# Copies of k on a second queue, logs summed earlier, half of the squares on another engine: a four-part edit of an attention and convolution trunk

## The chip, the cores and the metric

The kernel runs on one core of a Trainium2 chip. A core has TensorE (PE: matmuls, with results in eight PSUM banks of 128 x 512 float32), VectorE (DVE), ScalarE (ACT), GpSimd (POOL) and SyncE (SP), which here only issues DMAs; each engine works through its own instructions in order and waits on semaphores. Sixteen DMA engines move the data. The metric is the device time of one execution in microseconds (us), the median of several runs.

## The reference

Two layers over a sequence of 512 tokens with 1024 channels, all float32. Layer 0 mixes by attention with a forget gate, layer 1 by a short convolution; each layer then has a squared-ReLU MLP (4096 wide) and a gated embedding. Cut to what the change touches:

```
def rmsnorm(x, g):
    return x * rsqrt(mean(x * x) + 1e-6) * g

def fox_attention(h, w_in, b_f, w_out):          # h = rmsnorm(x, g[0])
    q, k, v, f_logit = split(h @ w_in)           # 16 heads of 64, and 16 gates
    c = cumsum(log_sigmoid(f_logit + b_f))       # over the 512 tokens
    s = (q / 8) @ k.T + c[query] - c[key]        # causal: -1e30 above the diagonal
    return (softmax(s) @ v) @ w_out
```

## The kernel before

All matmuls are made from a split of each float32 operand into a high and a low part: ScalarE writes the high part (`wh`, `xh`, `kh`, `hTh`) and VectorE the difference (`wl`, `xl`, `kl`, `hTl`); `mm3` then does three matmuls, high by high, high by low, low by high. Weights come by SyncE's queue into 14 buffers `raw` in a fixed order (`fetch`); a load waits until the splits of the weight 14 places before it have read its buffer.

The start of layer 0 goes like this. TensorE first makes v and the gates' logits from the raw x (chunk 0: 256 columns of v and the 16 gates; chunk 1: 512 columns; `values`: the last 256), with the norm applied afterwards: `inverse` takes the squares of token-major x (`xc`), gives `rs[t] = (mean + eps) ** -0.5` of each block t of 128 tokens, and `r_d`, its diagonal, from which `rows` makes the norm of every column. `logits` adds the gates' bias `b_f`, `logs` makes log sigmoids, and `sums_of_logs` their running sums by matmuls into `ps_c`. VectorE copies them out (`c_T`), makes `neg_c`, and SyncE writes that to memory. `normed_x` scales the two halves of x and splits them into `hTh` and `hTl`.

From these `project(i)` makes k and then q of a pair of heads. The scores of a head need k stacked twice, as high and low parts on 64 partitions each: a DMA copies `kh` and `kl` to the other half of the partitions (line 546), four copies for a pair. `bias(h)` loads `neg_c` of head h, one row for all partitions, in four DMAs (`prr`, `pr`, `prr`, `prl`, for the four blocks of queries, of 128 to 512 columns), which the scores are added to. After `project(0)` and most of the first half of `project(1)` the loop over heads begins: `scores` (lines 574 and 575), exponentials on ScalarE, transposes (`turn`), values (`mix`), with the projections of later pairs between them.

Up to the end of chunk 1 and `normed_x` the order of all engines is written out by hand; from `values` on a scheduler that works with estimated times sets it. DMAs tell of their landing on eight semaphores, `DMAHW0` to `DMAHW7`, which the scheduler gives out in turn, whichever queue issues the DMA; one that gets a semaphore waits until the DMA before it on that semaphore has landed.

Of the kernel before, what the change touches and what calls it, by code (L numbers as in the profile page):

```python
# [8 lines left out]
F32 = mybir.dt.float32  # L9
# [59 lines left out]
def trunk(ctx: ExitStack, tc, x, xT, pT, g, gT, wv, wqk, bf, wo, wci, wcq, cw, wco, wup, wdn, wpp, wpg, out):  # L69
# [16 lines left out]
    def stat(name, n=1, dtype=F32):  # L86
        return small.tile([P, n], dtype, tag=f"st{n}", name=name, bufs=32 if n == 1 else 8)
# [64 lines left out]
    def fetch(upto):  # L152
        while len(fetched) < min(upto, len(loads)):
            n = len(fetched)
            raw = raws.tile([P, S], F32, tag="raw", name=f"raw{n}")
            fetched.append(raw)
            src = loads[n]
            nc.sync.dma_start(raw[:, : src.shape[-1]], src)
# [164 lines left out]
    def stats(t, xs, name):  # L323
        return rstd([squares(xs[n][:, :S], f"{name}_q{n}_{t}") for n in range(2)], f"{name}_r{t}")
# [53 lines left out]
    def load_x(name, t):  # L378
        xs = [page(f"{name}{t}_{n}") for n in range(2)]
        for n in range(2):  # L380
            nc.sync.dma_start(xs[n][:, :S], x[t * P : (t + 1) * P, n * S : (n + 1) * S])
        return xs
# [29 lines left out]
    def attention(hT, raw_x, b_f, warm, work, by_hand):  # L412
# [31 lines left out]
        def sums_of_logs(tri):  # L444
            ps_c = bank("ps_c")
            for b in range(NB):
                for half in (lf.hi, lf.lo):
                    nc.tensor.matmul(
                        ps_c[:H, b * P :], half[:, b * H : (b + 1) * H], tri[:, : S - b * P],
                        start=b == 0 and half is lf.hi, stop=b == NB - 1 and half is lf.lo,  # L450
                    )
            c_T = page("c_T")
            nc.vector.tensor_copy(c_T[:H, :S], ps_c[:H, :])
            for b in range(NB):
                n = (b + 1) * P
                t = page(f"neg_c{b}")
                nc.vector.tensor_scalar(
                    out=t[:H, :n], in0=c_T[:H, :n], scalar1=c_T[:H, b * P : b * P + 1],
                    scalar2=-1.0, op0=ALU.subtract, op1=ALU.mult,
                )  # L460
                nc.sync.dma_start(neg_c[b, :, :n], t[:H, :n])
# [36 lines left out]
        def keep_values(c, t, ps):  # L498

            c0, width = V_CHUNKS[c]  # L500
            splits = []
            for c1 in range(0, min(width, D - c0), 256):
                i = (c0 + c1) // 256
                vs[t][i] = page(f"v{t}_{i}", F32R)
                src = ps[:, c1 : c1 + 256].rearrange("p (i e d) -> p i e d", e=2, d=HD)
                block = vs[t][i].rearrange("p (i r) -> p i r", i=2)
                for e in range(2):
                    hi = block[:, :, 192 * e : 192 * e + HD]
                    lo = block[:, :, 64 + 64 * e : 128 + 64 * e]
                    splits.append((hi, lo, src[:, :, e, :]))  # L510
            for hi, _, src in splits:
                nc.scalar.mul(hi, src, rs[t])
            for hi, lo, src in splits:
                nc.vector.scalar_tensor_tensor(
                    out=lo, in0=src, scalar=rs[t], in1=hi.bitcast(F32),
                    op0=ALU.mult, op1=ALU.subtract,
                )
# [3 lines left out]
        def project(i):  # L521

            heads = [[page(f"{n}{i}_{e}", F32R) for n in ("qs", "kh", "kl")] for e in range(2)]
            stacked[i] = heads
            for s in (1, 0):
                ps = bank(f"qk{i}_{s}")
                for k in range(KT):
                    mm3(
                        ps, narrow("qk", i, k=k, c=s * P),
                        hT.at(lambda h: h[:, k, :]), k == 0, k == KT - 1,  # L530
                    )
                    if k < KT - 1:
                        yield
                for e in range(2):
                    a, b = slice(64 * e, 64 * e + 64), slice(64 - 64 * e, 128 - 64 * e)
                    q, kh, kl = heads[e]
                    if s == 0:
                        nc.scalar.mul(q[a, :S], ps[a, :], HD**-0.5)
                        nc.vector.scalar_tensor_tensor(
                            out=q[b, :S], in0=ps[a, :], scalar=HD**-0.5,  # L540
                            in1=q[a, :S].bitcast(F32), op0=ALU.mult, op1=ALU.subtract,
                        )
                    else:
                        split(kh[a, :S], kl[a, :S], ps[a, :])
                        for h in (kh, kl):
                            nc.sync.dma_start(h[b, :S].bitcast(F32), h[a, :S].bitcast(F32))
                yield

        def bias(h):
# [144 lines left out]
        r_d = page("r_d")  # L694

        def inverse(t):
            rs[t] = stats(t, first_x[t], name)
            nc.gpsimd.tensor_scalar(
                out=r_d[:, t * P : (t + 1) * P], in0=ident, scalar1=rs[t], scalar2=None,
                op0=ALU.mult,  # L700
            )
# [10 lines left out]
        def normed_x(n, r_rows):  # L712

            halves = [raw_x[t][n][:, :S].rearrange("p (j c) -> p j c", j=4) for t in range(NB)]

            def low(t):
                to = lambda u: u[:, 4 * n : 4 * n + 4, t * P : (t + 1) * P]
                split(to(hT.hi), to(hT.lo), halves[t])

            for t, h in enumerate(halves):  # L720
                r = r_rows[:, t * P : (t + 1) * P].unsqueeze(1).to_broadcast([P, 4, P])
                nc.vector.tensor_tensor(out=h, in0=h, in1=r, op=ALU.mult)
                if t:
                    low(t - 1)
            low(NB - 1)

        with tc.manual_schedule(engines={E.PE, E.DVE, E.Activation, E.Pool, E.SP}):
            work(9)
            banks_v = {(0, t): bank(f"v0_{t}") for t in range(NB)}

            def halves(c, *at):
                for t, n in at:
                    if (c, t) not in banks_v:
                        banks_v[c, t] = bank(f"v{c}_{t}")
                    part(c, banks_v[c, t], t, n)

            split_x(0, 0)
            prepare(4)
            halves(0, (0, 0))
            split_x(0, 1)  # L740
            split_x(1, 0)
            halves(0, (1, 0))
            prepare(KT)
            fetch(2 * KT)
            first_x = [load_x("xc", t) for t in range(NB)]
            nc.sync.dma_start(b_f, bf[0:1, :].partition_broadcast(P))
            fetch(2 * KT + 4)
            halves(0, (0, 1))
            split_x(1, 1)
            halves(0, (1, 1))  # L750
            for t in (2, 3):
                for n in range(2):
                    split_x(t, n)
                    halves(0, (t, n))
            tri, ones = page("tri", F32R), page("ones")
            nc.gpsimd.memset(ones[:, :S], 1.0)
            nc.gpsimd.affine_select(
                out=ones[:, :S], in_=ones[:, :S], compare_op=ALU.is_ge, fill=0.0, base=0,
                pattern=[[1, S]], channel_multiplier=-1,
            )  # L760
            nc.vector.tensor_copy(tri[:, :S], ones[:, :S])
            prepare(KT + 4)
            halves(1, (0, 0), (1, 0))
            prepare(2 * KT)
            halves(1, (0, 1), (1, 1))
            for t in range(NB):
                inverse(t)
            halves(1, (2, 0))
            r_rows = rows()
            halves(1, (2, 1), (3, 0), (3, 1))  # L770
            for two in ((0, 1), (2, 3)):
                for t in two:
                    logits(t, banks_v[0, t])
                for t in two:
                    keep_values(0, t, banks_v[0, t])
                prepare(2 * KT + 4)
            steps = logs()
            next(steps)
            keep_values(1, 0, banks_v[1, 0])
            next(steps)  # L780
            keep_values(1, 1, banks_v[1, 1])
            next(steps)
            normed_x(0, r_rows)
            keep_values(1, 2, banks_v[1, 2])
            normed_x(1, r_rows)
            keep_values(1, 3, banks_v[1, 3])
        for t in range(NB):
            values(t)
            if t == 1:
                sums_of_logs(tri)  # L790
                bias(0)
                bias(1)
        for _ in project(0):
# [517 lines left out]
```

## Time and profile before

| | us |
|---|---|
| median of 3 runs (lowest, highest) | 1232.28 (1232.04, 1233.59) |
| the profiled execution | 1232.33 |
| its span, first to last instruction | 1230.4 |
| TensorE busy | 1209.3 (98%) |
| VectorE busy | 928.4 (75%) |
| ScalarE busy | 694.1 (56%) |
| GpSimd busy | 657.7 (53%) |

Times in the views count from the start of the span. A row of the timeline has the start, the time taken, engine, line, operation, output and inputs, and in brackets the idle time before it with what ended it; `SPq` is SyncE's queue, where the time is that of the issue and not of the transfer. A row of waits has the engine that waited, what it waited for, the total, how often, and the longest.

### The profile page before, as it was taken

How to read it: one execution, taken by the hardware profiler on the slowest of the kernel's cores; microseconds unless marked ns; L12 is line 12 of the kernel's file. 1: busy time of each engine (PE TensorE's matmuls, PEld its weight loads, DVE VectorE, ACT ScalarE, POOL GpSimd, SP SyncE). 2: the span in 40 equal slices, each digit the busy share in tenths (PEclk: the TensorE clock that was granted, in tenths of full speed). 3: DMA queues.
4: the chain of work that ended last, by engine and by line, in shares of the span. 5: the costliest groups of instructions: out<-in, count | busy, mean ns of one | idle time of the engine just before them, and what ended most of it. 6: DMA issues, size and time to landing. Idle time of an engine off the chain costs nothing.

```text
span 1230.4 us, 18747 instructions
## 1 busy us (share of the span) xinstructions
PE 1209.3 (98%) x6175; PEld 1030.8 (84%) x6175; DVE 928.4 (75%) x1462; ACT 694.1 (56%) x1473; POOL 657.7 (53%) x620
## 2 busy tenths in 40 slices
PE   9969999999999999999999999999999999999997
PEld 8858888798888888888889999989888888888886
DVE  5848888666787768869777798766776887669873
ACT  7747778647644644465567444445756345635551
POOL 2016566235877787866213255315677777778310
PEclk9979999999999999999999999999999999999999
DMA  9455554442443234328232132542422443245401
GB/s 317 138 149 165 154 168 132 143 167 66 124 138 94 83 97 137 120 62 287 80 104 86 52 100 98 155 154 96 129 73 73 138 137 94 61 121 169 174 8 61
DMA packets 87313, 150.83 MB, mean 123 GB/s; under 512 B 10352, under 2 KB 18080, under 8 KB 87216
## 3 DMA queue, kind: packets, MB, share of 16 engines
q1 hardware_dynamic: 86640, 149.11, 39.1%
q8 instruction: 49, 0.80, 0.3%
q10 hardware_dynamic: 576, 0.53, 0.1%
q14 instruction: 48, 0.39, 0.1%
HBM read 139.03 MB, written 6.37 MB: 118 GB/s over the span
## 4 chain that ended last, share of the span: by engine, by line
PE 88%; DVE 3%; issue 3%; ACT 2%; POOL 2%; DMA 1%; SPq 0%; POOLq 0%; ACTq 0%; DVEq 0%
PE up L270 9%; PE up L268 9%; PE up L269 9%; PE dn L268 8%; PE dn L270 8%; PE dn L269 8%; PE v L476 2%; PE qk L269 2%; PE qk L270 2%; PE qk L268 2%; PE pg L269 2%; PE pg L268 2%; PE pg L270 2%; PE pT L590 1%; PE co L270 1%
## 5 line engine op out<-in xcount | busy, mean ns | idle before, releaser
L277 DVE TENSOR_TENSOR wl<-raw,wh 128x512 fp32r<-128x512 f32 x346 | 345.2, 1043 | 14.6 <-ACT wh L276 13.9
L269 PE MATMUL up<-hTh,wl 128*128 128x512 f32 (+1 forms) x576 | 210.2, 365 | 0.0
L270 PE MATMUL up<-hTl,wh 128*128 128x512 f32 (+1 forms) x576 | 209.6, 365 | 0.0
L268 PE MATMUL up<-hTh,wh 128*128 128x512 f32 (+1 forms) x576 | 208.7, 366 | 0.0
L276 ACT CAST wh<-raw 128x512 fp32r<-128x512 f32 x346 | 189.4, 625 | 4.5 <-DVE xd L373 4.4
L966 ACT ACTIVATE r<-up 128x512 f32<-128x512 f32 (+1 forms) x72 | 39.4, 548 | 202.8 <-PE up L270 190.0
L277 POOL TENSOR_TENSOR wl<-dn_T,wh 128x512 fp32r<-128x512 f32 x96 | 132.7, 1416 | 30.0 <-ACT wh L276 30.0
L168 POOL TENSOR_TENSOR dn_T<-raw,raw 128x512 f32<-128x512 f32 x56 | 87.9, 1581 | 68.4 <-DMA raw<-in_wdn 49.5
L269 PEld LDWEIGHTS up<-hTh,wl 128*128 128x128 f32 x576 | 108.6, 189 | 17.6
L268 PEld LDWEIGHTS up<-hTh,wh 128*128 128x128 f32 x576 | 108.6, 188 | 17.5
L270 PEld LDWEIGHTS up<-hTl,wh 128*128 128x128 f32 x576 | 108.2, 188 | 17.4
L1012 DVE TENSOR_TENSOR acc<-dn,acc 128x512 f32<-128x512 f32 x168 | 107.5, 680 | 14.4 <-PE dn L270 14.2
L168 POOL TENSOR_TENSOR dn_T<-raw,dn_T 128x512 f32<-128x512 f32 x56 | 92.5, 1652 | 2.2
L276 ACT CAST wh<-dn_T 128x512 fp32r<-128x512 f32 x112 | 61.4, 616 | 10.9 <-POOL dn_T L168 10.9
L277 DVE TENSOR_TENSOR A12l<-q,A12h 128x512 fp32r<-128x512 f32 x28 | 22.8, 814 | 53.7 <-ACT A12h L276 53.7
L1026 POOL TENSOR_TENSOR acc<-acc,acc 128x512 f32<-128x512 f32 x28 | 46.9, 1708 | 9.9 <-DVE acc L1012 9.9
L269 PE MATMUL qk<-hTh,wl 128*128 128x512 f32 x128 | 51.2, 401 | 0.0
L270 PE MATMUL qk<-hTl,wh 128*128 128x512 f32 x128 | 51.2, 401 | 0.0
L268 PE MATMUL qk<-hTh,wh 128*128 128x512 f32 x128 | 50.9, 399 | 0.0
L277 DVE TENSOR_TENSOR A11l<-q,A11h 128x256 fp32r<-128x256 f32 x28 | 23.2, 827 | 36.5 <-ACT A11h L276 36.5
L269 PE MATMUL pg<-wh,hTl 128*128 128x512 f32 x128 | 50.5, 394 | 0.0
L268 PE MATMUL pg<-wh,hTh 128*128 128x512 f32 x128 | 50.4, 394 | 0.0
(400 smaller groups left out, 3311.3 us busy)
## 6 DMA issues: line engine op xcount, KB each, us to landing
raw<-in_wup SPq DMA_DIRECT2D x128, 256.0 KB, 3.0
raw<-in_wdn SPq DMA_DIRECT2D x128, 256.0 KB, 2.9
raw<-in_wcq SPq DMA_DIRECT2D x36, 256.0 KB, 2.8
raw<-in_wqk SPq DMA_DIRECT2D x32, 256.0 KB, 4.9
raw<-in_wpg SPq DMA_DIRECT2D x32, 256.0 KB, 4.5
g<-in_g SPq DMA_DIRECT2D x22, 256.0 KB, 5.3
prl<-neg_c SPq DMA_DIRECT2D x16, 256.0 KB, 6.5
raw<-in_wo SPq DMA_DIRECT2D x16, 256.0 KB, 4.5
```

The costliest lines, as they stand in the source:

```text
L168: ins = nc.gpsimd.tensor_tensor(out=B[name], in0=B[a], in1=B[b], op=op)
L268: nc.tensor.matmul(ps, a.hi, b.hi, start=start, stop=False)
L269: nc.tensor.matmul(ps, a.lo, b.hi, start=False, stop=False)
L270: nc.tensor.matmul(ps, a.hi, b.lo, start=False, stop=stop)
L276: nc.scalar.copy(hi, src)
L277: return eng.tensor_tensor(out=lo, in0=src, in1=hi.bitcast(F32), op=ALU.subtract)
L476: nc.tensor.matmul(ps[:, : V_CHUNKS[c][1]], getattr(of_x(k, t), p), getattr(ready["v", c, k], of), start=k == 0 and p == of, stop=k == KT ...
L590: nc.tensor.transpose(ps[:, b * P : (b + 1) * P], probs[h][b][:, j * P : (j + 1) * P], ident)
L966: nc.scalar.activation(r[:, :n], ps[:, :n], AF.Relu)
L1012: ins = nc.vector.tensor_tensor(out=a, in0=banks[s], in1=a, op=ALU.add)
L1026: nc.gpsimd.tensor_tensor(out=a, in0=a, in1=acc[i, s][:, :S], op=ALU.add)
```

## The change

It has four parts.

- The four copies of k of the first pair of heads (`i == 0`) are issued by ScalarE and no longer by SyncE.
- `sums_of_logs`, which stood behind `values(1)`, stands ahead of the second half of `normed_x`, in the stretch that is ordered by hand.
- The load of `b_f` stands ahead of the eight loads of token-major x.
- Of the two squares of each block, one stays on ScalarE (`squares`) and one goes to VectorE (`products`, with eps inside); VectorE adds the two, and GpSimd makes the power as before.

```diff
@@ project(i), s == 1
                         for h in (kh, kl):
-                            nc.sync.dma_start(h[b, :S].bitcast(F32), h[a, :S].bitcast(F32))
+                            eng = nc.sync if i else nc.scalar
+                            eng.dma_start(h[b, :S].bitcast(F32), h[a, :S].bitcast(F32))
@@
         def inverse(t):
-            rs[t] = stats(t, first_x[t], name)
+            half = lambda n: first_x[t][n][:, :S]
+            v = stat(f"{name}_v{t}")
+            q = squares(half(0), f"{name}_q0_{t}"), products(half(1), f"{name}_q1_{t}")
+            nc.vector.tensor_tensor(out=v, in0=q[0], in1=q[1], op=ALU.add)
+            rs[t] = stat(f"{name}_r{t}")
+            nc.gpsimd.tensor_tensor(out=rs[t], in0=v, in1=neg_half, op=ALU.pow)
@@
             fetch(2 * KT)
+            nc.sync.dma_start(b_f, bf[0:1, :].partition_broadcast(P))
             first_x = [load_x("xc", t) for t in range(NB)]
-            nc.sync.dma_start(b_f, bf[0:1, :].partition_broadcast(P))
@@
             keep_values(1, 2, banks_v[1, 2])
+            sums_of_logs(tri)
             normed_x(1, r_rows)
             keep_values(1, 3, banks_v[1, 3])
         for t in range(NB):
             values(t)
             if t == 1:
-                sums_of_logs(tri)
                 bias(0)
                 bias(1)
```

The scheduler orders all that follows anew. ScalarE's instructions before, from the last split of a weight to those that follow q of the first pair (`kh_0`, `kh_1`: the two heads; in brackets what a row waits for):

```order
L276 CAST kh_0_903<-qk_1_908 64x512 [waits PE_49]
L276 CAST kh_1_906<-qk_1_908 64x512 [waits DVE_49]
L538 ACTIVATE qs_0_902<-qk_0_973 64x512 [waits PE_49]
L538 ACTIVATE qs_1_905<-qk_0_973 64x512 [waits DVE_49]
L285 ACTIVATE wh_1009<-raw_1011,first_g 128x256 [waits DMAHW3_49,Activation_49]
```

and the same place now:

```order
L276 CAST kh_0_907<-qk_1_912 64x512 [waits PE_49]
L547 DMA kh_0_907<-kh_0_907 64x512 [waits DMAHW4_49,Activation_49]
L547 DMA kl_0_908<-kl_0_908 64x512 [waits DMAHW6_49,DVE_49]
L276 CAST kh_1_910<-qk_1_912 64x512
L547 DMA kh_1_910<-kh_1_910 64x512 [waits DMAHW7_49,Activation_49]
L538 ACTIVATE qs_0_906<-qk_0_977 64x512 [waits PE_49]
L547 DMA kl_1_911<-kl_1_911 64x512 [waits DMAHW0_49,DVE_49]
L538 ACTIVATE qs_1_909<-qk_0_977 64x512 [waits DMAHW5_49,DVE_49]
L285 ACTIVATE wh_1013<-raw_1015,first_g 128x256 [waits DMAHW3_49]
```

The four issues stand between the splits of k and q, and each waits for a landing on its semaphore besides its data.

SyncE's queue before, from the last two bias loads of head 1 (`neg_c`, the second of the two `prl`) to the copies; `in_wqk` are weights of later pairs, the first of them here raw42:

```order
L561 DMA prr_825<-neg_c 128x384
L561 DMA prl_824<-neg_c 128x512 [waits PE_49]
L158 DMA raw_1572<-in_wqk 128x512 [waits DMAHW1_49,DVE_49]
L158 DMA raw_1609<-in_wqk 128x512 [waits DMAHW2_49,DVE_49]
L158 DMA raw_1789<-in_wqk 128x512 [waits DMAHW3_49,DVE_49]
L546 DMA kh_0_903<-kh_0_903 64x512 [waits DMAHW4_49,Activation_49]
L158 DMA raw_1821<-in_wqk 128x512 [waits DMAHW5_49,DVE_49]
L546 DMA kl_0_904<-kl_0_904 64x512 [waits DMAHW6_49,DVE_49]
L546 DMA kh_1_906<-kh_1_906 64x512 [waits DMAHW7_49,PE_49,Activation_49]
L546 DMA kl_1_907<-kl_1_907 64x512 [waits DMAHW0_49,DVE_49,PE_49]
```

and now, from raw39 over the eight bias loads (heads 0 and 1) to raw42; the writes of `neg_c` stand six weights ahead of this, and the copies are gone:

```order
L158 DMA raw_1311<-in_wqk 128x512 [waits DMAHW6_49,DVE_49]
L562 DMA prr_811<-neg_c 128x128 [waits DMAHW7_49,PE_49]
L562 DMA pr_809<-neg_c 128x256 [waits DMAHW0_49,PE_49]
L562 DMA prr_811<-neg_c 128x384 [waits DMAHW1_49]
L562 DMA prl_810<-neg_c 128x512 [waits DMAHW2_49,PE_49]
L562 DMA prr_829<-neg_c 128x128 [waits DMAHW3_49,PE_49]
L562 DMA pr_809<-neg_c 128x256 [waits DMAHW4_49]
L562 DMA prr_829<-neg_c 128x384 [waits DMAHW5_49]
L562 DMA prl_828<-neg_c 128x512 [waits DMAHW6_49]
L158 DMA raw_1491<-in_wqk 128x512 [waits DMAHW7_49,DVE_49]
L158 DMA raw_1523<-in_wqk 128x512 [waits DMAHW0_49,DVE_49]
L158 DMA raw_1576<-in_wqk 128x512 [waits DMAHW1_49,DVE_49]
```

The bias loads moved ahead of raw40 and raw41. The semaphores show whom ScalarE's copies follow: the first kh (DMAHW4) the second load of head 1, the first kl (DMAHW6) its last load, the second kh (DMAHW7) raw40, the second kl (DMAHW0) raw41.

## The prediction

> **What bounds the kernel now.** I read the page first: TensorE is busy for 98% of the span. So I ask where it is not, in the view of waits, all of TensorE's:
>
> ```profile
> PE sc L574 <- DMA kh<-kh: 11.0, 1, 11.0
> ...
> PE sc L575 <- DMA kl<-kl: 0.7, 1, 0.7
> PE o L270 <- DVE wl L277: 0.3, 1, 0.3
> ```
>
> One wait of 11.0 us is nearly all there is once the start is over: the first score matmul waits for the copy of kh of the first pair of heads, and the next for the copy of kl. The timeline of TensorE, around it, and the windows (the clock is the seventh figure, behind the five engines):
>
> ```profile
> 71.96 0.39 PE L270 MATMUL qk<-hTl,wh 128*128 128x512 f32 x1
> 83.38 0.45 PE L574 MATMUL sc<-kh,qs 128*128 128x128 f32 x1 [11.03 <-DMA kh<-kh]
> 84.49 0.48 PE L575 MATMUL sc<-kl,qs 128*128 128x128 f32 x1 [0.66 <-DMA kl<-kl]
> ...
> 89.23 0.40 PE L268 MATMUL qk<-hTh,wh 128*128 128x512 f32 x1
> ...
> 75.00:80.00 5.00, 0.00 (x0) 0.00 (x0) 0.00 (x0) 0.00 (x0) 0.88 (x3) 0.54 0.83 216
> ...
> 85.00:90.00 5.00, 5.00 (x16) 4.14 (x16) 4.88 (x17) 3.58 (x10) 1.44 (x2) 0.59 0.48 122
> ```
>
> The clock drops during the wait and stays at half until about 89.2. From 72.2 (71.96 and 0.23, the distance between such matmuls at full clock: two take 0.63 in a row below, one 0.39) to 89.23 TensorE does eight score matmuls (2560 columns) and six of qk (3072): at 0.23 us per 512 columns that is 2.5 us of work in 17.0. **The stall with its clock is worth 14.5 us**, the most this change can give. Everything else is gaps of 0.3.
>
> Why do the copies come so late? SyncE's queue:
>
> ```profile
> 65.00 0.34 SPq L561 DMA_DIRECT2D prr<-neg_c  x1
> ...
> 68.99 0.78 SPq L561 DMA_DIRECT2D prl<-neg_c  x1
> 69.87 5.69 SPq L158 DMA_DIRECT2D raw<-in_wqk  x3
> 75.65 0.53 SPq L546 DMA_DIRECT2D kh<-kh  x1
> ...
> 77.00 0.70 SPq L546 DMA_DIRECT2D kl<-kl  x1
> ```
>
> and from the DMA view, one row for each of these issues (last figure: us to landing), and for the copies of all heads together:
>
> ```profile
> prr<-neg_c SPq DMA_DIRECT2D x1, 64.0 KB, 3.4
> ...
> prl<-neg_c SPq DMA_DIRECT2D x1, 256.0 KB, 10.5
> ...
> raw<-in_wqk SPq DMA_DIRECT2D x1, 256.0 KB, 10.6
> ...
> kh<-kh SPq DMA_DIRECT2D x1, 128.0 KB, 7.6
> ...
> kl<-kl SPq DMA_DIRECT2D x1, 128.0 KB, 7.4
> ...
> DMA to landing us min/median/max: 2.8/3.8/7.6
> ```
>
> Eight bias loads (two heads) land from 68.4 (65.00 + 3.4) to 79.5 (68.99 + 10.5): 11.1 us. The weights issued behind them land after them, and the copies after those: kh at 83.25, kl at 84.4. The first pair has the worst of all copies; 2.8 is the best.
>
> **The change part by part.**
>
> *Squares and gates' bias.* Now ScalarE does eight squares, and VectorE waits for b_f:
>
> ```profile
> 26.37 0.63 ACT L312 ACTIVATE junk<-xc 128x512 f32<-128x512 f32 x1
> 26.09 0.38 DVE L493 SCALAR_TENSOR_TENSOR logit<-v,n_r_y,b_f 128x16 f32<-128x16 f32 x2 [5.51 <-DMA b_f<-in_bf]
> 27.65 1.13 DVE L514 SCALAR_TENSOR_TENSOR v<-v,n_r_y,v 128x128 fp32r<-128x128 f32 x4 [1.19 <-ACT v L512]
> 90.48 0.69 DVE L577 CUSTOM_DVE_ANT_0 prl<-sc,prl 128x512 f32<-128x512 f32 x1
> ...
> xc<-in_x SPq DMA_DIRECT2D x2, 256.0 KB, 6.3
> ```
>
> Four of them go to VectorE; their nearest row is the reduction of the same shape at L577, 0.69 each. They fall into its idle 5.51 us, but all four, with their sums, stand ahead of the logits, and the last tile of x lands at about 25.8 (issued 19.4, 6.3 later), some 0.2 later with b_f ahead (estimate). So the logits come at about 27.0 instead of 26.09; the step behind them waits less (ScalarE has four squares fewer), and about 0.4 us of delay is left on VectorE. No gain: TensorE had no wait there, and b_f was late by less than this. Bounds: -0.5 to +1.
>
> *Sums of logs.* TensorE does the same eight matmuls earlier, the first ahead of the values of block 0, the rest among them. Their last input (lf_l) and the first of those values:
>
> ```profile
> 40.20 0.23 DVE L277 TENSOR_TENSOR lf_l<-logf,lf_h 128x64 fp32r<-128x64 f32 x1 [0.37 <-ACT lf_h L276]
> 43.12 0.28 PE L268 MATMUL v<-wh,xh 128*128 128x256 f32 x1
> ```
>
> 2.7 us lie between them, more than the 0.4 of delay above: nothing is charged, and if the logs came 3 us late TensorE would wait for 0.7. On VectorE:
>
> ```profile
> 53.61 6.03 DVE L287 SCALAR_TENSOR_TENSOR wl<-raw,first_g,wh 128x256 fp32r<-128x256 f32 x15
> 59.55 0.67 DVE L453 COPY c_T<-ps_c 16x512 f32<-16x512 f32 x1
> 61.58 1.25 DVE L457 TENSOR_SCALAR neg_c<-c_T 16x128 f32<-16x128 f32 x4
> 66.97 0.67 DVE L277 TENSOR_TENSOR kl<-qk,kh 64x512 fp32r<-64x512 f32 x1
> 55.84 0.63 PE L268 MATMUL qk<-hTh,wh 128*128 128x512 f32 x2
> ```
>
> 0.67 + 1.25 = 1.9 us go ahead of the second half of x, so the first wl starts at 53.61 + 1.9 + 0.4 = 55.9 and is there at 56.35, when TensorE wants it at 56.07: a stall of 0.3 us, which vanishes in the larger wait behind it. From the kl at 66.97 on VectorE has done the same work. The writes of neg_c leave earlier by more, ahead of the second half of x, but the bias loads stand in SyncE's order behind the loads of raw34 to raw39, and these wait for buffers that the wl give back: the sixth pair of wl is done at 55.9 + 6 x 0.8 = 60.7 (6.03 for fifteen). So the bias loads start at about 61.1 instead of 65.0, 3.9 earlier. They now follow weights in flight, where the queue was empty before (an estimate of up to 2.7 us), so their last lands between 75.6 and 78.3, and I take 77.0.
>
> *Copies on ScalarE's queue.* Two things hold them. First, the splits: on ScalarE
>
> ```profile
> 64.01 0.61 ACT L276 CAST kh<-qk 64x512 fp32r<-64x512 f32 x1
> 67.67 0.58 ACT L276 CAST kh<-qk 64x512 fp32r<-64x512 f32 x1 [3.06 <-DVE kl L277]
> 68.28 0.59 ACT L538 ACTIVATE qs<-qk 64x512 fp32r<-64x512 f32 x1
> 70.35 1.71 ACT L285 ACTIVATE wh<-raw,first_g 128x256 fp32r<-128x256 f32 x4
> 72.08 1.28 ACT L581 ACT_TABLE_LOAD   x1
> 85.46 0.40 ACT L581 ACTIVATE prr<-prr,nmx 128x128 f32<-128x128 f32 x1 [12.09 <-DVE nmx L577]
> ```
>
> the data of the first kl is there at 67.6 (66.97 + 0.67). Second, the semaphores. DMAs tell of their landing on eight semaphores in turn, and one that reuses a semaphore is issued when its predecessor has landed. The waits of SyncE show that this binds, by tiles with which the copies share nothing:
>
> ```profile
> SPq L546 <- DMA prl<-neg_c: 0.7, 1, 0.7
> SPq L546 <- DMA prr<-neg_c: 0.6, 1, 0.6
> ```
>
> In the changed order the first kh reuses the semaphore of the second bias load of head 1, the first kl that of the **last** bias load of head 1, the second kh that of raw40, the second kl that of raw41. So ScalarE, which works in order, stands at the first kl's issue until 77.0. That issue has 0.47 to 0.70, and the landing, behind nothing of its own queue but beside five weights on the other, takes 2.8 to 5.6 from the issue (the best copy; the last of the four above would be the nearest with company); I take 3.2, near the best, since no weight stands ahead: **80.2**. Meanwhile the queue of ScalarE: split of the second kh 0.6, its issue 0.5 (it waits for raw40, and the weight behind the last bias load landed 1.0 after it before, 69.87 + 10.6 against 79.5, so at 78), first qs 0.6, and VectorE's half of it 0.7: 79.9. The two meet; the score matmul that was at 84.49 comes at 80.2.
>
> At this place a rule of the Trainium skill speaks against the change: "DMA: Bandwidth & Descriptors", Issuing engines are not separate DMA queues, says that issuing from several engines saves only the sequencer's time, because the same 16 engines do the work. The rows differ: a copy's issue takes about 0.5, yet its landing 7.4 or 2.8, so most of the time is standing in line; and the page's Queues, rings and completion order has the engines take turns between queues, packet by packet, which agrees with that. By the first rule the sum would be the third case below.
>
> **Sum.** The profiled execution took 1232.33 for a span of 1230.4, and the median is 1232.28, so I work from 1232.3. The gap shrinks by 84.5 - 80.2 = 4.3; TensorE still idles for 7 us, so the half clock stays, with about as long a tail. The splits of weights and the table load (1.71 and 1.28) now come after the first scores and not in the long wait; the exponentials lag by 1 to 2 us, while the last transpose of the first block stands behind ten more matmuls of qk than before, 2.3 us: nothing charged, and without that cover 1 to 2 us. Four copies' issues, 2 us of ScalarE, are hidden in the wait. 1232.3 - 4.3 = **1228.0**. Its own range: 75.6 or 78.3 for the bias, 2.8 or 5.6 for the copy, and a tail of the clock shorter or longer by 1.5, give 1225 to 1230.5.
>
> **Rivals.**
> 1. *The stall goes altogether.* If the semaphores' predecessors land by 68, kl lands at about 71.5 and the scores follow at 72.2 without a drop of the clock: 1232.3 - 14.5 = 1217.8. For it: kl's data is ready at 67.6 and neg_c is written long before. Against it: the bias loads cannot be issued before 61, and took 11.1 us. Chance 0.13. Loads twice as fast give values between: 1221.5.
> 2. *Slower.* ScalarE now stands still for the copies, and behind them are qs, four splits of weights and the table load. If the last bias load lands after 81 (the series 15 us and not 11, with raw40 and later weights beside it), kl and qs come as late as before, and behind them stand the second q split 0.6, the splits 1.71 and the table load 1.28: the first exponential at 84.5 + 3.6 = 88.1 and not at 85.46. TensorE, in order, waits those 2.6 us at its transposes: 1235. Chance 0.12.
> 3. *No transfer gets faster.* The copies share the engines with the weights as before: kl landed 4.9 after the last bias load (84.4 - 79.5). With that load at the late end, 78.3, kl is there at 83.2: 1231.0. Chance 0.20.
>
> **How the numbers follow.** My case has 0.55. A measurement of this kernel tells 0.2%, 2.5 us, from no change: faster is below 1229.8. Of my case 0.52 lies there, with the first rival and a little of the third 0.68; same is most of the third and the rest, 0.22; slower 0.10. Range 1221.5 to 1232.5: it leaves out most of rivals 1 and 2.
>
> **What would show it.** TensorE's wait at L575/L576 for kl near 80 and 7 to 8 us long, with the clock at half behind it; ScalarE's copy issues at 72 to 79, the kl issue just behind the landing of head 1's prl; bias loads issued from about 61; VectorE's first wl near 55.9. I am wrong if the copies are issued before 70, if kl takes over 5 us to land, or if a new wait at the transposes (L591) shows.

## The result and the profile after

The changed kernel takes 1231.52 us (median of 12 runs, 1229.45 to 1232.70); the kernel before took 1231.86 beside it (12 runs, 1229.88 to 1233.59). The ratio is 0.9996, with a 95% interval of 0.9987 to 1.0005: no change that can be told. The forecast was 1228.0, in a range of 1221.5 to 1232.5; what came is half a microsecond from its third rival, 1231.0. The profiled execution of the changed kernel took 1232.70, the slowest of the twelve, with a span of 1231.0.

The view of waits, TensorE's rows at the place of the change and the two largest new ones:

```profile
PE sc L575 <- DMA kh<-kh: 7.5, 1, 7.5
PE sc L576 <- DMA kl<-kl: 2.2, 1, 2.2
...
PE qk L269 <- DVE wl L287: 0.4, 1, 0.4
PE pT L591 <- DVE pl L596: 0.4, 1, 0.4
```

The one wait of 11.0 us has become two, 9.7 us in all, where 7 to 8 was forecast. TensorE's timeline around them, and head 1's first score as a mark behind them:

```profile
72.74 0.39 PE L270 MATMUL qk<-hTl,wh 128*128 128x512 f32 x1
80.62 0.45 PE L575 MATMUL sc<-kh,qs 128*128 128x128 f32 x1 [7.49 <-DMA kh<-kh]
83.30 0.48 PE L576 MATMUL sc<-kl,qs 128*128 128x128 f32 x1 [2.23 <-DMA kl<-kl]
...
87.31 0.63 PE L575 MATMUL sc<-kh,qs 128*128 128x512 f32 x1
...
89.44 0.45 PE L268 MATMUL qk<-hTh,wh 128*128 128x512 f32 x1
...
91.56 0.22 PE L575 MATMUL sc<-kh,qs 128*128 128x128 f32 x1
```

The same mark in the kernel before:

```profile
91.55 0.22 PE L574 MATMUL sc<-kh,qs 128*128 128x128 f32 x1
```

The first score on kl starts 1.2 us earlier (83.30 against 84.49), but full speed is not back earlier (at 89.44 a row still takes 0.45, where before one took 0.40 at 89.23), and head 1's first score stands where it stood. Since the wait TensorE has by then done 18 matmuls of qk, where before it had done 16: two at 0.23 us, so 0.45 of the 1.2 us is left. The windows (the clock is the seventh figure, then the DMA engines' share and GB/s):

```profile
75.00:80.00 5.00, 0.00 (x0) 0.00 (x0) 1.27 (x2) 1.17 (x2) 0.58 (x2) 0.59 0.99 273
80.00:85.00 5.00, 2.15 (x7) 1.99 (x8) 1.88 (x7) 4.32 (x9) 0.00 (x0) 0.50 0.36 89
85.00:90.00 5.00, 5.00 (x14) 3.85 (x14) 4.79 (x17) 3.72 (x10) 2.15 (x3) 0.55 0.66 209
```

A mean of 0.59 is 4.1 us at half clock, 0.50 is 5, 0.55 is 4.5: 13.6 us. The same windows of before (0.54, 0.50, 0.59) give 13.7. And from 75 to 80, while the copies were on their way, the DMA engines were busy 99% of the time; before it was 83%.

ScalarE's timeline, where the copies are issued, and SyncE's, with the first and the last bias load and the weights behind them:

```profile
74.09 0.52 ACTq L547 DMA_DIRECT2D kh<-kh  x1
77.16 0.47 ACTq L547 DMA_DIRECT2D kl<-kl  x1
77.67 0.58 ACT L276 CAST kh<-qk 64x512 fp32r<-64x512 f32 x1 [10.21 <-DMA prl<-neg_c]
```

```profile
62.50 0.39 SPq L562 DMA_DIRECT2D prr<-neg_c  x1
...
68.35 0.45 SPq L562 DMA_DIRECT2D prl<-neg_c  x1
68.90 7.84 SPq L158 DMA_DIRECT2D raw<-in_wqk  x6
```

The DMA view, in narrow windows around these issues; the last figure is the time from issue to landing (the weight is the last of the six, issued at 76.4):

```profile
prr<-neg_c SPq DMA_DIRECT2D x1, 64.0 KB, 5.1
...
prl<-neg_c SPq DMA_DIRECT2D x1, 256.0 KB, 8.7
...
raw<-in_wqk SPq DMA_DIRECT2D x1, 256.0 KB, 6.6
...
kh<-kh ACTq DMA_DIRECT2D x1, 128.0 KB, 6.4
...
kl<-kl ACTq DMA_DIRECT2D x1, 128.0 KB, 6.1
```

The first bias load lands at 67.6 (62.50 + 5.1), the last at 77.1 (68.35 + 8.7), and ScalarE, which but for the issue of kh had stood for 10 us, issues kl at 77.16, right behind it. Then kl takes 6.1 us and lands at 83.25, though only kh, which landed at 80.5, is ahead of it in ScalarE's queue. The last weight, issued 0.8 us before it on the other queue, lands at 83.0.

### The profile page after: what moved, and what is told of

Read it like the earlier page. It is cut to its first block, busy times and chain, and to the rows that moved or that the text cites. A ratio compares the mean times of both kernels' runs of the same rounds, so it can differ in the third digit from the quotient of the medians.

```text
span 1231.0 us, 18748 instructions
## 1 busy us (share of the span) xinstructions
PE 1211.1 (98%) x6175; PEld 1031.8 (84%) x6175; DVE 928.9 (75%) x1474; ACT 691.1 (56%) x1465; POOL 653.7 (53%) x616
## 4 chain that ended last, share of the span: by engine, by line
PE 90%; DVE 2%; issue 2%; ACT 2%; DMA 2%; POOL 1%; SPq 0%; POOLq 0%; ACTq 0%; DVEq 0%
PE up L270 9%; PE up L268 9%; PE up L269 9%; PE dn L268 8%; PE dn L270 8%; PE dn L269 8%; PE v L476 3%; PE qk L269 2%; PE qk L270 2%; PE qk L268 2%; PE pg L269 2%; PE pg L268 2%; PE pg L270 2%; PE pT L591 1%; PE co L269 1%
```

## The experiments

Two theories at first. **S**: the semaphores' predecessors hold the copies back, and a copy that is issued early lands some 3 us later. **E**: a copy lands when the sixteen engines are through with what was issued before it, whichever queue that was on; only the order of issue counts. Later theories are named where they come up. Medians and ratios, each against the kernel before on the same chip:

| kernel | us (runs) | before | ratio (95%) |
|---|---|---|---|
| e1: before, copies alone | 1230.76 (10) | 1230.99 | 0.9995 (0.9985 to 1.0004) |
| e2: after, copies back on SyncE | 1231.23 (10) | 1230.99 | 1.0003 (0.9994 to 1.0012) |
| e3: after, eight weights behind the copies | 1226.14 (4) | 1230.99 | 0.9955 (0.9940 to 0.9970) |
| e4: copies on SyncE, head 1's bias and the weights behind | 1222.41 (4) | 1230.99 | 0.9929 (0.9914 to 0.9944) |
| e5: after, work in the wait | 1233.68 (10) | 1231.67 | 1.0012 (1.0002 to 1.0021) |
| e6: e3 with the copies on SyncE | 1225.02 (4) | 1231.67 | 0.9946 (0.9931 to 0.9961) |
| e7: after, five bias loads for a pair | 1226.97 (4) | 1231.67 | 0.9962 (0.9947 to 0.9977) |
| e8: e4 and e7 together | 1219.49 (4) | 1231.67 | 0.9901 (0.9886 to 0.9916) |
| e9: e5 with GpSimd's order mended | 1229.03 (10) | 1231.94 | 0.9979 (0.9969 to 0.9988) |
| e10: e8 without the change's four parts | 1219.04 (4) | 1231.94 | 0.9896 (0.9881 to 0.9911) |

**e1, the copies alone.** The kernel before with the first part of the change only:

```diff
+                            eng = nc.sync if i else nc.scalar
+                            eng.dma_start(h[b, :S].bitcast(F32), h[a, :S].bitcast(F32))
```

> The kernel before with the first part of the change alone: the first pair's copies on ScalarE's queue. Theory S (the copies are held by the landing of the DMA that had their semaphore before, and take about 3 us once issued) has kl wait for the second bias load of head 1 (75.6 in the profile before), so issue near 75.7, landing near 79, first scores near 79.5: some 4 to 5 us faster, 1227 to 1228. Theory E (a copy lands when the 16 engines are through with what was issued before it, whichever queue it is on) has it land with raw45 near 83.5 to 84: 1231 to 1232.5, no change.

1230.76, between the two forecasts and not to be told from before. TensorE's timeline:

```profile
79.23 0.45 PE L575 MATMUL sc<-kh,qs 128*128 128x128 f32 x1 [8.02 <-DMA kh<-kh]
81.08 0.47 PE L576 MATMUL sc<-kl,qs 128*128 128x128 f32 x1 [1.40 <-DMA kl<-kl]
```

9.4 us of waits instead of 11.7: this part alone does about what the whole change does.

**e2, all but the copies.** The changed kernel with its first part undone:

```diff
-                            eng = nc.sync if i else nc.scalar
-                            eng.dma_start(h[b, :S].bitcast(F32), h[a, :S].bitcast(F32))
+                            nc.sync.dma_start(h[b, :S].bitcast(F32), h[a, :S].bitcast(F32))
```

> The changed kernel with the copies back on SyncE's queue; the other three parts stay. The copies' semaphores have the same predecessors as in the changed kernel (the last bias load of head 1 for kl). Theory S: ScalarE no longer stands still, but kl is issued at about 77.2 behind raw44 and raw45, lands 3 to 4 us later than in the changed kernel: near 85 to 86, some 2 to 3 us slower than the changed one, 1234. Theory E: kl lands where it did, 83 to 84, so 1231 to 1232.5.

1231.23, as E had it. S had it slower than before, and falls here: without the copies on ScalarE nothing is lost (kl lands at 82.8 in its profile, 0.5 us earlier than in the changed kernel). The other three parts together bring nothing either.

**e3, the weights behind the copies.** The changed kernel, with the loads of raw40 to raw47 ordered behind the first pair's copies. The copies' semaphores then follow those of head 0's bias loads:

```diff
+            if 40 <= n < 48 and copies:
+                behind(ins, copies[-1])        # order only, no wait
```

> The changed kernel with the order of semaphores altered: the weights raw40 to raw47 are ordered behind the first pair's copies, so that the copies follow the bias loads of head 0 on their semaphores (kl the second of them, landing near 69) and the weights follow the bias loads of head 1 and the copies. The copies stay on ScalarE's queue, the bias loads of both heads stand ahead in time as before. Theory S: kl issued near 69, landing near 72 to 73, the wait of TensorE shrinks to 0 to 1 us without a drop of the clock: 1218 to 1220. Theory E: kl lands when the bias loads issued before it are through, near 77: the wait shrinks to about 5 us, the clock drops and comes back one step (3.4 us) earlier: 1225 to 1227.

1226.14, E's forecast. The copies' issues on ScalarE, and then landings from the DMA view (the last bias load, issued at 65.8, and kl):

```profile
66.11 0.52 ACTq L553 DMA_DIRECT2D kh<-kh  x1
67.36 0.47 ACTq L553 DMA_DIRECT2D kl<-kl  x1
```

```profile
prl<-neg_c SPq DMA_DIRECT2D x1, 256.0 KB, 9.2
...
kl<-kl ACTq DMA_DIRECT2D x1, 128.0 KB, 8.2
```

The copies are issued 8 to 10 us earlier than in the changed kernel, which was S's whole point, and now take 8.2 us: kl lands at 75.6, just behind the bias load at 75.0. The early issue alone did not bring the 3 us that S had; standing ahead of the weights is what moved the landing.

**e6, the same on SyncE's queue.** If a queue of its own let the copies take turns with the bias loads (theory **Q**), this had to be slower than e3.

```diff
-                            eng = nc.sync if i else nc.scalar
+                            eng = nc.sync
```

> As e3 (weights raw40 to raw47 behind the first pair's copies), but with the copies on SyncE's queue. Theory E (a copy lands when the 16 engines are through with what was issued before it, whichever queue it is in): the same order of issue, so the same time as e3, 1226.1, within 1 us, and kl landing 0 to 1 us behind the last bias load of head 1. Rival Q (a queue of their own lets the copies take turns with the bias loads): 2 us or more slower than e3, 1228 to 1230.

1225.02 against 1226.14, measured on two chips; the intervals of the two ratios overlap. SyncE's issues, and landings:

```profile
66.69 0.89 SPq L570 DMA_DIRECT2D prl<-neg_c  x1
...
68.67 2.80 SPq L553 DMA_DIRECT2D kl<-kl  x1
```

```profile
prl<-neg_c SPq DMA_DIRECT2D x1, 256.0 KB, 8.7
...
kl<-kl SPq DMA_DIRECT2D x1, 128.0 KB, 7.9
```

kl lands at 76.6, 1.2 us behind the bias load (75.4). The order is the same and the time is no longer: on which queue the copies stand makes no difference that can be told, and Q falls.

**e4, the copies ahead of head 1's bias too.** All first-pair copies on SyncE; head 1's bias loads and raw40 to raw47 behind them. To e6 it adds:

```diff
                 bias(0)
-                bias(1)
         for _ in project(0):
             pass
+        bias(1)
...
+                if h == 1 and copies:
+                    behind(ins, copies[-1])        # in bias
```

> The changed kernel with the copies on SyncE's queue, and both the bias loads of head 1 and the weights raw40 to raw47 ordered behind them: ahead of the copies stand only the four bias loads of head 0. Both theories have kl issued near 68.8 (its data is there at 68.7) and landing near 72 to 73: TensorE's wait 0 to 1 us, no drop of the clock, 1217 to 1220, unless the bias loads of head 1, then landing near 81, make the scores of head 1 wait: up to 4 us more. If it does not get faster than 1226, the copies are not the cause of the stall.

1222.41, above the 1217 to 1220 that both theories gave, and not for the reason that was named as possible, the bias of head 1. TensorE's timeline, and the DMA view for the second pair's kh, issued at 80.70:

```profile
72.28 0.22 PE L585 MATMUL sc<-kh,qs 128*128 128x128 f32 x1
72.34 0.28 PE L586 MATMUL sc<-kl,qs 128*128 128x128 f32 x1
...
88.08 0.30 PE L585 MATMUL sc<-kh,qs 128*128 128x128 f32 x1 [2.35 <-DMA kh<-kh]
```

```profile
kh<-kh SPq DMA_DIRECT2D x1, 128.0 KB, 7.3
```

The first wait is gone: scores at 72.28, with no drop of the clock. But the weights that were moved back now stand ahead of the next pair's copies, and kh lands at 88.0. The wait returns one pair later, 2.35 us long.

**e7, fewer bias loads.** Eight loads of 64 to 256 KB become five of 256 KB, the same 1280 KB: blocks 2 and 0 side by side in memory, and block 1 of both heads. Theory **P**: a load costs by its packets; **B**: by its bytes.

```diff
+            for to, src in (
+                (rest[:, :], neg_c[2, h : h + 1, :]),           # blocks 2 and 0
+                (both[i][:, :], neg_1[2 * i : 2 * i + 2, :]),   # block 1, with head e == 0
+                (long[:, :S], neg_c[3, h : h + 1, :]),
+            ):
```

> The changed kernel with five bias loads for a pair of heads in place of eight, the same 1280 KB: the rows of blocks 2 and 0 lie side by side in DRAM and so do the rows of block 1 of both heads, so that each load fills 128 rows of 2 KB. Theory P (a broadcast load costs by its packets, about 1.4 us for 64 KB as for 256 KB): three loads fewer are 4.2 us off the series; the copies land 4 us earlier, kl near 79, and TensorE's wait is about 5.5 us: 1227 to 1228.5. Theory B (it costs by its bytes): 1231 to 1232.

1226.97, at the edge of P's forecast and far from B's. The DMA view for the first and the last bias load (issued at 61.50 and 63.36), then kl on ScalarE's queue (issued at 72.72):

```profile
prr<-neg_c SPq DMA_DIRECT2D x1, 256.0 KB, 7.0
...
prl<-neg_c SPq DMA_DIRECT2D x1, 256.0 KB, 9.3
...
kl<-kl ACTq DMA_DIRECT2D x1, 128.0 KB, 6.2
```

The series ends at 72.7 and not at 77.1, 4.4 us earlier (4.2 expected); but 1.0 of this is an earlier start (61.50 against 62.50), so the loads themselves are worth 3.4: 11.2 us from the first issue to the last landing, and not 14.6. kl is issued at once again and again takes 6.2 us, behind the weights. So the bytes do not decide; that the packets do, as P has it, is not shown (see the last section).

**e8, both together.** e4's order with e7's loads.

> e4 (first pair's copies on SyncE ahead of head 1's bias loads and of raw40 to raw47) with the five bias loads of e7. Theory P: the first wait stays away, head 1's series has two loads and raw41 to raw47 and the second pair's copies come about 4 us earlier, kh before 85.5 where TensorE wants it, so the wait of 2.35 us that e4 has at 85.7, and its step at half clock, go as well: 1217.5 to 1219.5. Theory B: as e4, 1222.4.

1219.49, 12.2 us less than before. The copies' landings (kh issued at 66.36, kl at 67.61), and TensorE's windows:

```profile
kh<-kh SPq DMA_DIRECT2D x1, 128.0 KB, 2.8
...
kl<-kl SPq DMA_DIRECT2D x1, 128.0 KB, 2.2
```

```profile
75.00:80.00 5.00, 5.00 (x26) 4.25 (x25) 3.07 (x11) 3.09 (x9) 2.97 (x6) 1.00 1.00 361
80.00:85.00 5.00, 5.00 (x25) 3.93 (x23) 3.55 (x13) 4.22 (x12) 2.00 (x2) 1.00 1.07 235
85.00:90.00 5.00, 4.34 (x25) 3.57 (x24) 4.14 (x15) 4.23 (x13) 2.54 (x7) 1.00 1.02 291
```

With only the end of head 0's bias loads ahead of it, a copy takes 2.2 to 2.8 us. TensorE is busy for 14.3 of these 15 us and the clock stays at 1.00.

**e10, e8 without the change.** The same two edits on the kernel before.

> e8 without the other three parts of the change: the kernel before, with five bias loads for a pair and the first pair's copies ahead of head 1's loads and of raw40 to raw47. If the parts are worth nothing once the copies stand first: 1219.5, as e8. If the earlier bias loads matter (in before they were issued from 65.0, in the changed kernel from 61.3): head 0's three loads then land near 70 and the copies near 71 to 73, kh wanted at 72.2, a wait under 1 us: 1219.5 to 1221.5. Slower than 1222 would say that the parts carry a share of e8's gain.

1219.04, as e8. The three parts of the change that e8 has carry no share of its gain, and the fourth, the copies on ScalarE, is not in it.

**e5, work in the wait.** The changed kernel with 36 matmuls, which nobody reads, ahead of the first score, to keep the clock up:

```diff
+                for _ in range(36):
+                    ins = nc.tensor.matmul(idle, hT.hi[:, 0, :P], hT.hi[:, 1, :], start=True, stop=True)
+                    behind(ins, tail[0])           # the last matmul of qk, then one another
+                    tail[0] = ins
```

Theory **T**: the half clock behind the wait is a cost of its own.

> The changed kernel with 36 matmuls of 512 columns, whose result nobody reads, ahead of the first score matmul: 36 x 0.23 = 8.3 us of work in the wait, nothing else. Theory T (the half clock behind the wait is a cost of its own, as long however long the wait is): kl still lands at 83.3, the clock stays full, and the 6.25 us that the changed kernel spends at half clock after 83.30 become half as long: 3.1 us less, 1228.4 (2 to 4 us less). Rival (the matmuls behind the scores wait for their operands anyway): 1230.5 to 1232.

1233.68, slower, against both sides of the forecast. Its stage read on TensorE's and GpSimd's timelines:

```profile
72.34 8.32 PE L580 MATMUL idle<-hTh 128*128 128x512 f32 x36
...
82.37 0.33 PE L586 MATMUL sc<-kl,qs 128*128 128x128 f32 x1 [0.90 <-DMA kl<-kl]
...
84.55 0.39 PE L583 MATMUL sc<-kh,qs 128*128 128x512 f32 x1
```

```profile
91.36 0.29 POOL L565 TENSOR_SCALAR_AFFINE_SELECT pr<-pr 128x128 f32<-128x128 f32 x1 [0.91 <-DMA pr<-neg_c]
91.64 0.60 POOL L594 TENSOR_SCALAR prr<-prr,rs 128x128 f32<-128x128 f32 x1
```

The largest wait of TensorE's:

```profile
PE pT L601 <- POOL prr L594: 3.2, 1, 3.2
```

The clock was kept: the score of the fourth block starts at 84.55, where the changed kernel had it at 87.31. But the scheduler, which reckoned with the 36 matmuls, had put masks of head 2's bias ahead of head 0's normalisation on GpSimd, and TensorE waited for that at its transposes. There the clock fell after all: the windows from 95 to 105 have 6.9 us at half. The run says nothing on T's price at the end.

**e9, the same with that order mended.** Head 2's masks are held behind head 1's second normalisation (and head 3's behind its last):

```diff
+            if c == -3:
+                bias(2)                            # was at c == -4
...
+                if h in (2, 3):
+                    behind(sel, tail[1])           # sel: the mask; tail[1]: the last normalisation
```

> e5 again (36 unread matmuls in the wait of the changed kernel), with the masks of head 2's bias held behind head 1's second normalisation on GpSimd, which in e5 had slipped ahead of head 0's and made TensorE wait 3.9 us at its transposes. Theory T: the half clock behind the wait costs about 3 us of its own (in e5 the matmuls of the stream behind it stood 3.8 us earlier than in the changed kernel, 0.9 of which came from kl landing earlier), and with no new wait it reaches the end: 1228 to 1229. Rival (the work behind was held by operands and gives it back): 1230.5 to 1232.

1229.03, which is 2.5 us below the changed kernel, at the edge of T's forecast (against before on its own chip: 2.9 less, where the changed kernel had 0.3 less). In eight of the ten executions the clock over the whole span was 0.999, where the changed kernel has 0.993 to 0.995; they took 1227.54 to 1230.66. The profiled execution is not one of them; it was the slowest, 1232.08, with 0.996:

```profile
84.12 0.48 PE L588 MATMUL sc<-kl,qs 128*128 128x128 f32 x1 [3.60 <-DMA kl<-kl]
```

kl landed late in it, the matmuls had run out, and the clock fell after all.

## Why the prediction was right or wrong, point by point

- **What bounds the kernel**: right. With the waits gone (e8, e10) 12 to 13 us were won, of the 14.5 the stall was worth.
- **Squares and gates' bias**: no gain, right, as far as e2 tells for the three parts together. The first rows on VectorE came a little later than worked out:

```profile
27.67 0.38 DVE L493 SCALAR_TENSOR_TENSOR logit<-v,n_r,b_f 128x16 f32<-128x16 f32 x2
41.18 0.23 DVE L277 TENSOR_TENSOR lf_l<-logf,lf_h 128x64 fp32r<-128x64 f32 x1 [0.37 <-ACT lf_h L276]
56.45 6.42 DVE L287 SCALAR_TENSOR_TENSOR wl<-raw,first_g,wh 128x256 fp32r<-128x256 f32 x16
```

  The logits are at 27.67 (27.0 worked out), and 1.0 us of delay is left at lf_l, not 0.4.
- **Sums of logs**: the first wl is at 56.45 (55.9 worked out), TensorE's stall for it is 0.4 us (0.3), and the first bias load is issued at 62.50 (61.1). The last lands at 77.1 where 77.0 was taken, and that is luck: the start was 1.4 us later than worked out, and from the first issue to the last landing the series took 14.6 us, as before (14.5), where the prediction had added 1.4 for the weights in flight, out of a bound of 2.7 that no row gives.
- **What holds the copies**: right to 0.2 us. kl's issue stands until the last bias load has landed, 77.16.
- **The landing of kl: the step that failed.** 3.2 us was taken, "since no weight stands ahead" in its own queue. It took 6.1, over the upper bound of 5.6, and over the 5 us named as the mark of being wrong. The six weights issued ahead of it on SyncE's queue all landed before it. That is 2.9 us of the forecast 4.3. Nor was its own queue empty: kh, issued 3 us earlier, took 6.4 us, and its landing at 80.5 alone would have kept the scores from starting at 80.2. e3 and e6 show that the order of issue, and not the queue, decides.
- **The tail of the half clock**: "about as long" was too short. From the first score on kl the clock stayed at half for 6.2 us (83.3 to 89.5), where before it was 4.6 (84.5 to 89.1). These 1.6 us, a little more than the 1.5 that the prediction allowed for, cost half as much in work, 0.8 us, and of the 1.2 us that the scores came earlier 0.45 was left at head 1's first score.
- **What of it reached the end**: not settled. The medians differ by 0.34, and the interval allows from 1.6 us less to 0.6 more. The profiled execution has a clock of 0.994 over its span, as before; nine of the twelve executions have 0.995 (of the 45 of the kernel before that ran beside e1 to e10, five), so most probably spent less time at half clock than the one in the profile. Yet those nine took 1229.45 to 1232.59, no less than before, and where the rest went no trace shows.
- **The sum and its range**: taken together the upper bounds, 78.3 and 5.6, put kl at 83.9 and the time at 1231.7, so the 1230.5 that the prediction gave for its own case was too narrow; kl at 83.25 came before that 83.9, though its own 6.1 is over its bound. The forecast of 1228.0 is 3.5 us too low, and the gain did not come. The stated range, 1221.5 to 1232.5, holds 1231.52 because it took in the third rival.
- **The rivals**: the third is what happened, by its mechanism. Its place for kl, 83.2, is right by luck: the last bias load came 1.2 us earlier than it had (77.1, not 78.3), and the landing behind it took 1.2 us longer (6.1, not 4.9). The second did not come: the wait at the transposes is 0.4 us.

The Trainium skill says in "DMA: Bandwidth & Descriptors", Issuing engines are not separate DMA queues, that issuing from several engines saves the sequencer's time alone. The prediction weighed this and set it aside; e1 (1230.76 against 1230.99) and the pair e3 and e6 (1226.14 and 1225.02) agree with it. The prediction took what the Trainium skill says on the same page, of engines that take turns between queues, packet by packet (Queues, rings and completion order), as a reason for a quicker landing. In the traces of all these kernels no copy of the first pair landed more than 0.7 us ahead of a transfer whose issue began half a microsecond or more before its own, so turns of that kind, if the engines take them, are worth little here.

## What to carry to other kernels

A transfer that was late behind others was not helped by another queue here: count what is issued ahead of it on all queues, and move it ahead, or make what is ahead smaller. When it is moved, look at which transfer is then the last in line (e4). And a wait that is long enough to bring the clock down costs its tail of half clock too, so part of it may be worth little: here the first 2.0 us off the wait of 11.7 brought nothing that can be told, and with all of it gone the time fell by 12.2 (e8).

## What was not expected of the hardware

The time at half clock behind the wait came in steps of 3.4 us. From the windows of each profiled execution, as above: 13.7 in before and 13.6 in the changed kernel (waits of 11.7 and 9.7 us), 10.3 in e1 and 10.2 in e2 (9.4 and 10.0), 6.8 in e3 and e7 (3.4 and 5.9), 3.4 in e4, at the second pair, and e6 (2.7 and 3.3), none in e8 and e10: four, three, two, one and no steps. So one or two microseconds off such a wait can leave the time at half clock as it was in one execution and take a step of 3.4 us off it in another. The Trainium skill has this in "TensorE: Matmul & The Clock Gate", What's actually happening: a free-running window of about 3.4 us decides; the traces agree in the size of the step.

Loads of one row to all partitions were slow, and not by their bytes: on average 1.4 us from one landing to the next as eight of 64 to 256 KB ((77.1 - 67.6) / 7), 1.0 as five of 256 KB ((72.7 - 68.5) / 4), with the same bytes in all. The averages hide more. The DMA view of the changed kernel for the last two of the eight, issued at 68.35 and at 67.29:

```profile
prl<-neg_c SPq DMA_DIRECT2D x1, 256.0 KB, 8.7
prr<-neg_c SPq DMA_DIRECT2D x1, 192.0 KB, 9.1
```

The load of 256 KB landed 0.7 us behind that of 192 KB (77.1 and 76.4), and this one 2.3 us behind the load of 128 KB before it (74.0). So a count of loads does not explain it either, and what does is open.
